# One flag for the instruction scheduler of a two-layer decoder trunk

## The chip, the cores and the metric

The kernel runs on one core of a Trainium2 chip. The metric is the device time of one execution in microseconds. Before the change the median is 2463.65 us over two runs (2462.15 and 2465.15).

## What is computed

The reference is a decoder trunk of two layers over 1024 tokens of width 1024, all in float32. Each layer normalises, mixes tokens in two ways side by side on 512 columns each, projects and adds; then a squared-ReLU MLP of width 4096 follows.

```python
for i in range(DEPTH):                      # DEPTH = 2
    u = rms_norm(h, norm_mix[i])
    if i % 2 == 0:  mix = mixer_fox_ssd(u, ...)   # forgetting attention (8 heads of 64) || Mamba-2 SSD
    else:           mix = mixer_sb_gla(u, ...)    # stick-breaking attention (8 heads) || gated linear attention
    h = h + mix
    u = rms_norm(h, norm_mlp[i])
    h = h + squared_relu_mlp(u, w_mlp_up[i], w_mlp_down[i])
return rms_norm(h, norm_final)
```

Forgetting attention (FoX here) is a softmax of scores plus a running sum of log gates. Stick-breaking attention multiplies the sigmoid of a score by the product of one minus the sigmoids of the later keys. SSD and gated linear attention (GLA) carry a state from chunk to chunk.

## The kernel before, in words

Every float32 product is made of three matmuls on numbers split into a high and a low half: `split` (L78 on ACT, L79 on DVE) writes a rounded copy and the remainder, and `projA` (L146 to L158, matmuls on L156) and `mulB` (L165 to L174, matmuls on L172) multiply high by high, high by low and low by high over eight blocks of 128 rows. One product of 128 by 512 is thus 24 matmuls into one bank of PSUM.

In order of time, with the times of the profile, the stages are: norm and value projection (to 67 us), forgetting attention (67 to 281), convolution projections of SSD (to 365), the SSD loop over eight chunks (to 475), output projection (to 548), MLP (to 1195; up part at L414, down part at L572), value projection of layer 1 (to 1247), stick-breaking attention (1262 to 1495), GLA projections (to 1590), GLA (to 1730), output projection (to 1800), MLP (to the end).

Both attentions run through `attend` (L222). It takes four pairs of heads. For each pair it projects queries and keys (`qk_pair`, 96 matmuls on L156 in four groups of 24), and then goes through four phases, two heads by two halves of the rows. A phase makes scores (L248 and L250, from the split keys `kh` and `kl` into a bank `sc`), probabilities (`rows`, on DVE, ACT and POOL, into tiles `pr`), and for the phase before it `weigh`: transposes (L273, into a bank `tr`), a split of them (L78, L79), and the product with the values (L265, into the bank `av`):

```python
for p in range(4):
    qkt = self.qk_pair(w, p * P, HF + p * P)
    for e in range(2):
        for hf in (1, 0):
            probs = self.scores(qkt, 2 * p + e, e, hf, rows)
            if last: self.weigh(pool, v, catT, *last)
            last = (p, e, hf, probs)
```

Queries and keys have one buffer each, so that the projections of a pair may run while the pair before it is still in work, but their results are written only when its last score has been made. In stick-breaking attention a row of 128 queries goes through two sigmoids on ACT (L874, L875), masks on POOL (L879), a running product on DVE (L881) and a multiplication on DVE (L882). In this text **stretch A** of a pair runs from the last score of the pair before to the last score of the pair's own first phase; **stretch B** holds the remaining three phases.

GLA handles each half of the tokens in two blocks of heads; each block goes through eight levels (`intra`, 16 small matmuls on L966 into two banks `sc`, then two copies under a mask on DVE, L973; before them L983 to L990 make the operands on POOL, ACT and DVE), and then four chunks follow (L1005 to L1043). Each chunk also needs a gate, 24 matmuls on L172 with weights `zw`, which depends on nothing in the levels. The SSD loop has gate products of the same kind.

PSUM has eight banks, handed out by name: three `mm` (projections, gates), two `sc`, two `tr`, one `av`.

The program is written as one list of instructions. The framework puts them into an order for each engine with a list scheduler: it models how long each instruction takes and what it waits for, and at each step picks one that could start. Each engine then works through its own list in that order, and waits on semaphores where an operand or a buffer isn't ready. So which matmuls stand between two scores is the scheduler's decision, not the program's.

## Time and profile before

| | us |
|---|---|
| median of the runs | 2463.65 |
| profiled execution, its own time | 2468.61 |
| its span | 2466.9 |
| TensorE busy in the span | 2386.3 (97%) |
| DVE busy | 1651.6 (67%) |
| ACT busy | 1285.7 (52%) |

The profile is of one execution; its own time stands 5 us over the median of the runs. Busy time of TensorE (PE) is modelled from the ends of pipelined matmuls, and a PE that is busy isn't PE at its peak. The stages differ in what limits them, so the rows below are taken by stretches.

### The profile page before, as it was taken

The page shows a single profiled execution, that of the slowest core. Times are in us where ns is not written, and L with a number is a line of the kernel's source. Part 1 is how long each engine was busy: PE and PEld are TensorE (multiplying, and loading weights), DVE is VectorE, ACT ScalarE, POOL GpSimd, SP SyncE. Part 2 cuts the span into 40 slices and gives each one's busy share as a digit, 9 for nine tenths or more (in the row PEclk, how much of TensorE's full clock was granted, in tenths as well). Part 3 has the DMA queues.
Part 4 walks back from the last instruction along what each step waited for, and adds up shares of the span by engine and source line. Part 5 has one row for each costly group of instructions (what it writes and reads, how often), then busy time and mean ns, then how long its engine had stood idle before and what let it go on. Part 6 is the DMA issues. An engine that isn't in the chain of part 4 may idle for free.

```text
span 2466.9 us, 35276 instructions
## 1 busy us (share of the span) xinstructions
PE 2386.3 (97%) x12350; PEld 1949.8 (79%) x12350; DVE 1651.6 (67%) x2972; ACT 1285.7 (52%) x2502; POOL 220.0 (9%) x310
## 2 busy tenths in 40 slices
PE   8999998999999999999998889999999999999998
PEld 7777776897888887888876668777988888888886
DVE  5687766557566658667659885577386655578567
ACT  4476636435555543445546664654155555544445
POOL 1011102100000000000013331122000000000000
PEclk9999998899999999999999999999999999999999
DMA  5211323203444478567511111101404444587576
GB/s 143 61 57 54 102 54 78 73 22 116 141 142 155 163 275 277 146 223 224 172 35 27 27 35 44 44 10 38 134 22 154 160 152 145 192 304 236 166 225 214
DMA packets 251586, 310.85 MB, mean 126 GB/s; under 512 B 24432, under 2 KB 148352, under 8 KB 251408
## 3 DMA queue, kind: packets, MB, share of 16 engines
q1 hardware_dynamic: 251408, 308.60, 39.2%
q8 instruction: 97, 1.59, 0.3%
q14 instruction: 81, 0.66, 0.1%
HBM read 237.16 MB, written 71.37 MB: 125 GB/s over the span
## 4 chain that ended last, share of the span: by engine, by line
PE 78%; issue 7%; DVE 6%; DMA 3%; POOL 3%; ACT 2%; SPq 0%; POOLq 0%; DVEq 0%; ACTq 0%
PE tr L414 14%; PE mm L572 10%; PE mm L172 9%; PE mm L156 8%; PE sc L414 7%; PE mm L414 5%; PE sc L572 5%; PE tr L572 5%; PE sc L172 4%; PE av L572 3%; PE sc L966 2%; PE av L172 2%; PE av L265 1%; PE tr L273 1%; DVE rr L881 1%
## 5 line engine op out<-in xcount | busy, mean ns | idle before, releaser
L78 ACT CAST wh<-f 128x512 fp32r<-128x512 f32 (+1 forms) x384 | 224.3, 585 | 404.8 <-PE av L572 162.6
L79 DVE TENSOR_TENSOR wl<-f,wh 128x512 fp32r<-128x512 f32 (+1 forms) x384 | 246.6, 643 | 166.6 <-ACT wh L78 163.6
L79 DVE TENSOR_TENSOR wl<-raw,wh 128x512 fp32r<-128x512 f32 (+1 forms) x340 | 233.4, 689 | 123.4 <-ACT wh L78 119.5
L78 ACT CAST wh<-raw 128x512 fp32r<-128x512 f32 (+1 forms) x340 | 209.4, 619 | 178.8 <-PE mm L414 47.0
L156 PE MATMUL mm<-U,wh 128*128 128x512 f32 x832 | 279.3, 404 | 0.0
L172 PE MATMUL mm<-wh,U 128*128 128x256 f32 (+2 forms) x992 | 227.8, 313 | 0.2 <-ACT U L78 0.2
L414 PE MATMUL tr<-E,wh 128*128 128x512 f32 x720 | 225.5, 394 | 0.0
L156 PEld LDWEIGHTS mm<-U,wh 128*128 128x128 f32 x832 | 156.8, 191 | 31.6 <-issue 0.8
L123 POOL TENSOR_TENSOR rs<-ms,mhalf 128x1 f32<-128x1 f32 (+2 forms) x56 | 41.8, 748 | 1552.8 <-DVE ms L121 1552.8
L172 PEld LDWEIGHTS mm<-wh,U 128*128 128x128 f32 x992 | 163.4, 190 | 14.6 <-issue 4.0
L156 PE MATMUL mm<-U,wl 128*128 128x512 f32 x416 | 167.9, 404 | 0.0
L414 PEld LDWEIGHTS tr<-E,wh 128*128 128x128 f32 x720 | 135.4, 188 | 31.7
L172 PE MATMUL mm<-wl,U 128*128 128x256 f32 (+2 forms) x496 | 154.3, 311 | 0.6 <-DVE wl L79 0.6
L572 PE MATMUL mm<-wl,wh 128*128 128x512 f32 x384 | 152.3, 397 | 0.3 <-DVE wl L79 0.2
L572 PE MATMUL mm<-wh,wh 128*128 128x512 f32 x384 | 151.4, 394 | 0.0
L572 PE MATMUL mm<-wh,wl 128*128 128x512 f32 x384 | 151.2, 394 | 0.0
L414 PE MATMUL sc<-U,wh 128*128 128x512 f32 x480 | 150.4, 394 | 0.0
L414 PE MATMUL tr<-E,wl 128*128 128x512 f32 x360 | 141.9, 394 | 0.0
L78 ACT CAST ph<-tr 128x512 fp32r<-128x512 f32 x192 | 88.7, 487 | 64.0 <-PE tr L273 62.3
L273 PE MATMUL tr<-ident,pr 128*128 128x128 f32 x576 | 96.9, 278 | 21.2 <-DVE pl L79 16.0
L172 PE MATMUL sc<-wh,U 128*128 128x256 f32 (+1 forms) x560 | 108.7, 285 | 0.2
L414 PE MATMUL mm<-U,wh 128*128 128x512 f32 x304 | 99.3, 405 | 8.2 <-ACT U L78 7.1
(343 smaller groups left out, 5638.1 us busy)
## 6 DMA issues: line engine op xcount, KB each, us to landing
raw<-in_w_mlp_down SPq DMA_DIRECT2D x192, 256.0 KB, 3.8
raw<-in_w_mlp_up SPq DMA_DIRECT2D x128, 256.0 KB, 3.5
q<-in_w_mlp_down SPq DMA_DIRECT2D x64, 512.0 KB, 4.7
f<-hidS SPq DMA_DIRECT2D x128, 256.0 KB, 2.9
hidS<-q SPq DMA_DIRECT2D x96, 256.0 KB, 3.0
hidA<-f SPq DMA_DIRECT2D x64, 256.0 KB, 3.2
f<-hidA SPq DMA_DIRECT2D x64, 256.0 KB, 2.9
raw<-in_w_in_ab SPq DMA_DIRECT2D x40, 256.0 KB, 3.0
```

The lines of the kernel that those rows point to most:

```text
L78: self.nc.scalar.copy(hi, src)
L79: self.nc.vector.tensor_tensor(out=lo, in0=src, in1=hi.bitcast(F32), op=ALU.subtract)
L123: nc.gpsimd.tensor_tensor(rs, ms, self.mhalf[:, :w], op=ALU.pow)
L156: nc.tensor.matmul(ps, a, b[hf][:, kc], start=kc == 0 and i == 0, stop=kc == NKC - 1 and i == 2)
L172: nc.tensor.matmul(d, a, b, start=kc == 0 and i == 0, stop=kc == NKC - 1 and i == 2)
L265: nc.tensor.matmul(av[:, o:], v[j][:, h], x[:, o:], start=j == 0 and k == 0, stop=j == nj - 1 and k == 1)
L273: nc.tensor.transpose(ps[:, k * P:(k + 1) * P], probs[k][:, j * P:(j + 1) * P], self.ident)
L414: nc.tensor.matmul(ps, a[:, kc], b[:, kc], start=new and kc == 0 and i == 0, stop=kc == 3 and i == 2, skip_group_check=True)
L572: nc.tensor.matmul(ps[j], l[:, cs], r, start=own is not None and k == 0 and x == 0, stop=k == NG - 1 and x == 2, skip_group_check=True)
L881: nc.vector.tensor_tensor_scan(s, s, s, 1.0, ALU.mult, ALU.bypass)
L966: nc.tensor.matmul(ps[hh][:, c], kx[rows, cs], qx[rows, cs], start=True, stop=True)
```

## The change

The context in which the program is scheduled gets one flag. The traced program is the same; the list scheduler takes its durations and waits from the framework's other timing model.

```diff
-    with tile.TileContext(nc) as tc:
+    with tile.TileContext(nc, schedule_with_timeline_sim=True) as tc:
         trunk(tc, *args)
```

What it changes is the order on each engine. ACT has two fewer loads of its function table (36 for 38); the instructions are otherwise the same ones. POOL's order differs in a few places, and SP, which issues the DMAs, has its issues moved by at most about 26 places.

In both attentions the projections of the next pair are placed otherwise. The first place is PE in stretch B of stick-breaking attention, between two pieces of scores of a phase (`sc_13681` and `sc_13741` are banks of scores; `mm_13930` is a projection of the next pair). Before:

```order
L248 MATMUL sc_13681<-kh_3005_13212,qs_3003_13210 128x512
L250 MATMUL sc_13681<-kl_2856_12574,qs_3003_13210 128x512
L265 MATMUL av_13697<-ph_13703,v_12082 128x512
L156 MATMUL mm_13930<-U_76,wh_13897 128x512
L156 MATMUL mm_13930<-U_76,wl_13898 128x512
L156 MATMUL mm_13930<-U_76,wh_13897 128x512 x2
L156 MATMUL mm_13930<-U_76,wl_13898 128x512
L156 MATMUL mm_13930<-U_76,wh_13897 128x512
L248 MATMUL sc_13741<-kh_3005_13212,qs_3003_13210 128x128
L250 MATMUL sc_13741<-kl_2856_12574,qs_3003_13210 128x128
```

With the change, from the same score on:

```order
L248 MATMUL sc_13681<-kh_3005_13212,qs_3003_13210 128x512
L250 MATMUL sc_13681<-kl_2856_12574,qs_3003_13210 128x512
L265 MATMUL av_13533<-ph_13606,v_12089 128x128
L265 MATMUL av_13533<-pl_13607,v_12089 128x128
L273 MATMUL tr_13707<-ident_69,pr_3057_13494 128x128
L273 MATMUL tr_13707<-ident_69,pr_3060_13508 128x128
L273 MATMUL tr_13707<-ident_69,pr_3063_13522 128x128
L248 MATMUL sc_13741<-kh_3005_13212,qs_3003_13210 128x128
L250 MATMUL sc_13741<-kl_2856_12574,qs_3003_13210 128x128
L273 MATMUL tr_13715<-ident_69,pr_3060_13508 128x128
L273 MATMUL tr_13715<-ident_69,pr_3063_13522 128x128
```

The five projections that stood between the two scores are gone; transposes of the phase before stand there. All over stretch B it is 34 projections before and none now.

The second place is PE in stretch A, around the first score of the next pair (`sc_14036`). Before:

```order
L273 MATMUL tr_14119<-ident_69,pr_3133_13786 128x128
L156 MATMUL mm_14577<-U_76,wh_14567 128x512
L248 MATMUL sc_14036<-kh_3164_13887,qs_3162_13885 128x128
L156 MATMUL mm_14577<-U_76,wh_14567 128x512
L156 MATMUL mm_14577<-U_76,wl_14568 128x512
L156 MATMUL mm_14577<-U_76,wh_14567 128x512
L250 MATMUL sc_14036<-kl_2855_12573,qs_3162_13885 128x128
L248 MATMUL sc_14052<-kh_3164_13887,qs_3162_13885 128x512
L250 MATMUL sc_14052<-kl_2855_12573,qs_3162_13885 128x512
```

With the change:

```order
L156 MATMUL mm_14577<-U_76,wl_14568 128x512
L156 MATMUL mm_14577<-U_76,wh_14573 128x512 x2
L156 MATMUL mm_14577<-U_76,wl_14574 128x512
L156 MATMUL mm_14577<-U_76,wh_14573 128x512 x2
L156 MATMUL mm_14577<-U_76,wl_14574 128x512
L156 MATMUL mm_14577<-U_76,wh_14573 128x512 x2
L248 MATMUL sc_14036<-kh_3164_13887,qs_3162_13885 128x128
L156 MATMUL mm_14577<-U_76,wl_14574 128x512
L156 MATMUL mm_14577<-U_76,wh_14573 128x512
L250 MATMUL sc_14036<-kl_2855_12573,qs_3162_13885 128x128
```

The projections (`mm_14577`) now stand in blocks of one piece ahead of the score and between its two matmuls, where one to three stood before. Over a stretch A of stick-breaking attention it is 62 projections before (50 in the second pair's) and 96 now; in forgetting attention 68 and 96 in stretch A, 28 and none in stretch B. In the last pair of stick-breaking attention, which has no next pair, 75 more value projections of GLA (L172, 264 columns) stand inside the stage, and 54 instead of 129 behind it.

The third place is PE in GLA's levels (`sc_16205` to `sc_16241` are banks of levels, `mm_16472` is a gate product). Before, three gate matmuls stand between every two levels:

```order
L966 MATMUL sc_16205<-gM_16199 128x128
L966 MATMUL sc_16206<-gM_16199 128x128
L172 MATMUL mm_16472<-wh_16121,U_76 128x512
L172 MATMUL mm_16472<-wl_16122,U_76 128x512
L172 MATMUL mm_16472<-wh_16121,U_76 128x512
L966 MATMUL sc_16223<-gM_16217 128x128 x3
L966 MATMUL sc_16224<-gM_16217 128x128 x3
L966 MATMUL sc_16223<-gM_16217 128x128
L966 MATMUL sc_16224<-gM_16217 128x128
```

With the change a whole gate product of 24 stands ahead of each of the first levels of a half (`mm_16548` is one), and none from the sixth on; these are later levels:

```order
L966 MATMUL sc_16331<-gM_16325 128x128 x4
L966 MATMUL sc_16332<-gM_16325 128x128 x4
L966 MATMUL sc_16349<-gM_16343 128x128 x4
L966 MATMUL sc_16350<-gM_16343 128x128 x4
L966 MATMUL sc_16367<-gM_16361 128x128 x4
L966 MATMUL sc_16368<-gM_16361 128x128 x4
L966 MATMUL sc_16385<-gM_16379 128x128 x4
L966 MATMUL sc_16386<-gM_16379 128x128 x4
L966 MATMUL sc_16403<-gM_16397 128x128 x4
L966 MATMUL sc_16404<-gM_16397 128x128 x4
```

Nothing but the levels' own matmuls is left between these levels, where three gate matmuls stood. In the SSD loop the gate products move forward in the same way: 45 and 43 of the 512-column matmuls stand in the steps after the first two chunks, and 12 of 256 columns in each later step. In the MLPs the first product of a group is moved ahead of the later products of the group before it.

## Rows read from the trace of the kernel before

**Rows 1.** The page: span, busy time, granted clock of PE in 40 slices

```profile
span 2466.9 us, 35276 instructions
...
PE 2386.3 (97%) x12350; PEld 1949.8 (79%) x12350; DVE 1651.6 (67%) x2972; ACT 1285.7 (52%) x2502; POOL 220.0 (9%) x310
...
PEclk9999998899999999999999999999999999999999
```

**Rows 2.** Windows: length, busy PE, PEld, DVE, ACT, POOL, clock, DMA share, GB/s

```profile
178.50:207.00 28.50, 28.19 (x144) 22.07 (x143) 20.96 (x50) 19.38 (x39) 2.11 (x5) 1.00 0.23 66
207.00:229.60 22.60, 22.29 (x125) 17.61 (x124) 20.52 (x68) 18.73 (x43) 5.54 (x11) 1.00 0.13 38
1368.50:1399.50 31.00, 27.95 (x138) 20.73 (x137) 25.47 (x46) 20.09 (x43) 7.31 (x15) 1.00 0.13 35
1399.50:1429.20 29.70, 25.65 (x130) 18.31 (x129) 28.95 (x44) 21.13 (x50) 15.85 (x18) 1.00 0.07 19
600.00:900.00 300.00, 300.00 (x1294) 242.90 (x1293) 176.92 (x274) 163.22 (x275) 0.00 (x0) 1.00 0.49 163
381.60:464.60 83.00, 78.49 (x390) 57.42 (x390) 61.88 (x122) 53.85 (x129) 25.35 (x25) 0.89 0.24 58
...
430.50:437.20 6.70, 4.41 (x19) 2.37 (x18) 2.65 (x9) 5.01 (x11) 3.84 (x4) 1.00 0.25 46
437.20:444.00 6.80, 6.80 (x26) 5.97 (x25) 4.78 (x8) 4.13 (x12) 1.09 (x1) 0.50 0.21 33
...
1260.00:1495.00 235.00, 207.66 (x1067) 154.88 (x1065) 206.57 (x332) 157.95 (x352) 85.63 (x127) 1.00 0.10 27
1590.00:1730.00 140.00, 136.50 (x959) 105.22 (x957) 99.39 (x207) 68.16 (x182) 34.85 (x33) 1.00 0.10 30
```

**Rows 3.** Windows of one pair of each attention, projections on L156 alone

```profile
178.50:207.00 28.50, 18.25 (x69) 12.68 (x69) 1.00 0.23 66
207.00:229.60 22.60, 8.30 (x28) 4.85 (x27) 1.00 0.13 38
1368.50:1399.50 31.00, 16.99 (x62) 11.05 (x61) 1.00 0.13 35
1399.50:1429.20 29.70, 10.75 (x35) 6.59 (x36) 1.00 0.07 19
```

**Rows 4.** Chain of waits in saturated stretches: start, length, what ran

```profile
602.92 5.58 PE tr L414 x24
...
1207.52 2.85 PE mm L172 x24
```

**Rows 5.** PE in time, three GLA levels and the gate matmuls between two

```profile
1600.11 1.67 PE L966 MATMUL sc<-gM 64*128 64x128 f32 x16
1601.70 0.50 PE L172 MATMUL mm<-wh,U 128*128 128x512 f32 x1
1602.04 0.39 PE L172 MATMUL mm<-wl,U 128*128 128x512 f32 x1
1602.27 0.40 PE L172 MATMUL mm<-wh,U 128*128 128x512 f32 x1
1602.60 1.59 PE L966 MATMUL sc<-gM 64*128 64x128 f32 x16
...
1605.02 1.65 PE L966 MATMUL sc<-gM 64*128 64x128 f32 x16
```

**Rows 6.** Groups of DVE, 1589.5 to 1628.7: busy, mean ns of one, idle

```profile
L973 DVE COPY_PREDICATED v<-kl,sc 128x512 f32<-128x512 int32 x27 | 18.2, 728 | 0.4 <-PE sc L966 0.4
L988 DVE TENSOR_TENSOR gM<-gM,v 128x256 f32<-128x256 f32 x14 | 5.9, 424 | 5.1 <-ACT gM L986 5.1
L990 DVE TENSOR_TENSOR gM<-gM,v 128x256 f32<-128x256 f32 x14 | 5.9, 420 | 0.0
```

**Rows 7.** Waits of PE: us in total, times, longest

```profile
PE tr L273 <- DVE pl L79: 16.0, 22, 1.5
PE mm L414 <- ACT U L78: 7.1, 4, 2.7
```

**Rows 8.** PE in time ahead of a fall of the clock, SSD loop

```profile
435.81 0.48 PE L786 MATMUL sc<-CT,BT 64*128 64x128 f32 x2 [1.94 <-DVE tmp L810]
```

## Prediction, made before the changed kernel was run

> **What bounds the kernel now.** I read the page first: PE is busy 2386.3 of a span of 2466.9 us, 97%, DVE 67%, ACT 52%, and PE's granted clock is near full in almost every slice [rows 1]. An order can't remove work, so what it can win is limited by PE time that isn't work. For that I priced PE's matmuls by stretches in which they stand back to back: 24 matmuls of 512 columns took 5.58 us, 0.232 each, and 24 of 256 columns 2.85 us, 0.119 each [rows 4]. Transposes and matmuls of 128 columns cost 0.10 to 0.11: sixteen in 1.59 to 1.67 us [rows 5].
>
> Next come the windows by stage [rows 2]. In 300 us of the MLP PE is busy for 300.00: whatever stands in whatever order there, the sum is the same. In forgetting attention PE is busy 28.19 of 28.50 and 22.29 of 22.60, so PE sets the pace in both stretches. In stick-breaking attention it is otherwise: in stretch A PE has 27.95 of 31.00 and DVE 25.47, in stretch B DVE has 28.95 of 29.70, 97%, and PE waits 4.05 us. Over the whole stage PE is idle 27.3 us of 235 [rows 2], and the waits name DVE's split of the transposed probabilities, 16.0 us in 22 waits [rows 7]. The SSD loop leaves PE idle 4.5 us of 83, and one stretch of 6.80 us ran at clock 0.50 [rows 2]. GLA leaves 3.5 of 140 [rows 2].
>
> So three stages have a second engine near its limit beside PE, and the filler (projections and gates that wait for nothing in the stage) is what lets PE and DVE be busy at the same time. Of projections the stretches hold 62 and 35 in stick-breaking attention, 69 and 28 in forgetting attention [rows 3].
>
> **The change, part by part.** It removes no matmul and adds none (the two table loads of ACT that go cost nothing gained, ACT being 52% busy [rows 1]). It moves filler. The moved order gives in stick-breaking attention 96 projections in stretch A and none in stretch B. I price each stretch by the larger of PE's work and DVE's.
>
> *Stick-breaking attention.* PE's work in A: 62 projections by 0.232, 14.4 us, and 11.1 us of scores, transposes and values, 25.5 before; with 96, 22.3 + 11.1 = 33.4. In B: 34 by 0.232, 7.9, and 14.4 of its own, 22.3 before; 14.4 after. DVE's work, at what its instructions take undisturbed, is some 20 in A and 27 to 29 in B, little changed. By the larger of the two, a pair takes 25.5 + 27.0 = 52.5 before and 33.4 + 29.1 = 62.5 after: 10 us more. But a pair is measured at 31.0 + 29.7 = 60.7 now [rows 2], so that it already pays 8.2 us of waits. If the new order has none of these, 62.5 is only 1.8 us more than 60.7. That is the lower bound of a boundary between pairs, 10 the upper one. There are three boundaries: +5 to +30. In the last pair the 75 GLA matmuls of 264 columns, 9.2 us by the 0.119 of 256 columns scaled, fill B's idle PE and are missing behind the stage: between 0 and -9.2. Together -4 to +30. I take 6 us for each boundary, the middle, because the 16.0 us of waits on DVE [rows 7] are a chain (transpose, split, values) that a block of filler doesn't shorten, and half of the 9.2; the first boundary gains 46 projections where the others gain 34, 2.8 us more, half of it taken: 18 - 4.6 + 1.4, **+15**.
>
> *Forgetting attention.* PE's work in A goes from 27.0 to 32.2, in B from 20.7 to 15.8, where DVE's 20.5 [rows 2] to 21.4 then decides. The larger-of sum goes from 48.4 to 53.6, +5.2 a boundary; against the measured 51.1 it is only +1.6 to +2.5. Three boundaries: +5 to +16, and +2 at the upper end for the first pair, whose first phase holds 72 projections in blocks. I take **+13**, near the upper end, since PE is saturated here now [rows 2] and has no waits to give up, and what 51.1 has over 48.4 will stay.
>
> *SSD loop.* The gate products come in large blocks after the first two chunks and thinly later. The larger-of sum over the chunks grows by 9; at the best PE's 4.5 us of gaps and 3.4 us (half of the 6.80 at clock 0.50) go away. Bounds -8 and +10; **+2**, because the chain between chunks and not the amount of filler makes the gaps.
>
> *GLA.* DVE needs two copies of 0.728 and two products of 0.42, 2.30 us, for a level [rows 6]; PE 1.67 for a level's matmuls and 0.7 for three gate matmuls [rows 5]. Before they are even. In the eleven levels that lose their filler PE waits for DVE, 2.30 - 1.67 = 0.63 each, 6.9 us; in the first five a block of 24 costs PE 5.6 and DVE waits. What the chunk part wins back, since its gates are already made, is at most the 3.5 us of idle [rows 2]. Bounds -3 and +11 (6.9 and as much again over a part of the second half); **+4**.
>
> *MLPs and joins.* The MLPs stay saturated. At the joins PE waits 7.1 us in four waits for the first split operand, the longest 2.7 [rows 7]; the next group's first product ahead of them may cover that. Bounds -9 (the 7.1 and some idle at a smaller join) and +6 (two more waits like the longest); **-2**. SP's issues move a little; the DMA share of the windows is 0.07 to 0.49 [rows 2], so that a transfer a few issues later is hidden by what is loaded ahead; without that cover it would be one more wait like the 2.7, within the +6.
>
> *The clock.* At 437 us the granted clock fell to 0.50, the lower of the two levels (1.2 GHz), for 6.8 us, after a stretch in which PE was busy 4.41 of 6.70 us [rows 2] and had waited 1.94 us at once [rows 8]. Stretch B of stick-breaking attention keeps 1.00 at 25.65 of 29.70 now; after the change it has 14.4 us of work in 29, and GLA's later levels 1.67 in 2.30. Such a fall costs half of 6.8, 3.4 us, where PE then sets the pace, as in the block that follows, and nothing where DVE does. Two falls that count: **+7**, bounds 0 and, with seven, +25.
>
> Sum: 15 + 13 + 2 + 4 - 2 + 7 = +39, with all lower ends -19 and all upper ends +100. The profiled execution is 2468.6 us, so 2507.6; it stands 5 us over the median, so **2503 us** for a median.
>
> **Rivals.** *The clock falls at most of the thin stretches.* For it: there is one fall after a stretch 66% busy [rows 2], and B would be at 50%. There are about twelve places (the ends of the four stretches B of each attention, two halves of GLA, two steps of SSD): twelve times 3.4 is 41, less the 7 in the sum, so 2503 + 34 = 2537. Against it: in all of the stick stage, with 27.3 of 235 us idle, the windows show 1.00. The Trainium skill ("TensorE: Matmul & The Clock Gate", A second HAM failure mode: psum-queue depth-cycling) says that frequent short idles of PE between groups of matmuls suffice to make the clock go back and forth. By that rule the stick stage before would already do so; its rows at 1.00 speak against it, the SSD rows for it.
>
> *The blocks are paid by waits that are there already.* The place is stretch A of stick-breaking attention: if DVE has 5.6 us of finished scores to work on (one block of 24 by 0.232) whenever a block of projections begins, it never starves, and the 8.2 us of waits of a pair vanish. From that point on all blocks go to their lower ends: stick -4, FoX +5, SSD -8, GLA -3, joins -2, clock 0: -12, or 2452. For it: B is already 97% DVE, so that taking filler out of it can cost nothing there. Against it: only two banks hold scores, and in A DVE is already idle 5.5 of 31.0 us with 62 projections. The skill's rule ("Perfetto Trace Analysis", Identifying the Most-Contended Engine) is to judge PE's headroom by the busy share of weight loads; here that is 20.73 of 31.0, 0.67, in stretch A against 242.90 of 300, 0.81, in the MLP, which would leave 4.4 us of room in A for the extra projections (31.0 times the difference of the shares). That speaks for this rival.
>
> *The known terms at their upper ends* without the clock: 2503 + 5 + 8 + 15 + 7 + 8 = 2546.
>
> **How the numbers follow.** Forecast 0.50 (0.40 of it within 2%, 0.10 above); the clock 0.26 (0.22 slower, 0.04 within); the blocks paid by old waits 0.18 (0.15 within, 0.03 faster, where the joins and the SSD loop give more too); upper ends 0.06 (0.05 slower). 2% of 2463.65 is 49 us, 2414 and 2513, about what a measurement of this kernel can tell from no change. Faster 0.03, within 0.60, slower 0.37. The range goes from 2446, which takes in the second rival and a little more at the joins, to 2550, which takes in the clock's 2537 and the upper ends. The forecast's own range is 2480 to 2525.
>
> **What the profile after would show.** In stick-breaking attention a stretch A of about 34 to 36 us with 96 projections and PE nearly always busy, DVE idle more than now, and a stretch B of about 29 with PE idle for half of it. In forgetting attention A near 32, B near 21. In GLA periods of 2.3 us for the later levels, and 7 for the first. The MLP windows unchanged at 300 of 300. The clock at 0.50 in parts of stretch B would tell for the first rival; a pair of 60 us or less in stick-breaking attention for the second. I would be wrong if the MLPs moved, if B took more than 31 us, for then the chain and not DVE's work sets it, or if A had its projections without DVE waiting.

## The result and the profile after

The changed kernel takes 2579.4 us, median of two runs (2578.29 to 2580.51), against 2463.65 before: a ratio of 1.047, interval 1.0425 to 1.0515, or 116 us slower. The forecast was 2503 with a range up to 2550. It had the right sign and a third of the size.

The page of the changed kernel, its span, busy time and the granted clock, answering to [rows 1]:

```profile
span 2578.8 us, 35337 instructions
...
PE 2435.6 (94%) x12350; PEld 2023.5 (78%) x12350; DVE 1673.3 (65%) x2972; ACT 1285.0 (50%) x2500; POOL 211.1 (8%) x310
...
PEclk9999999699999999999999889977898999999999
```

The span grew by 111.9 us. PE's idle time went from 80.6 us (2466.9 less 2386.3) to 143.2, and the row of the clock has dips that it did not have. The mean clock fell from 0.989 to 0.956. Since the clock has two levels, 1.00 and 0.50, the time at half clock is twice the missing share: 0.022 of 2466.9 us, 54 us, before and 0.088 of 2578.8, 227 us, now, in 30 stretches instead of 8. PE loses at most half of that time: 27 us before, 113 now, 86 more. What can be seen of it is less: the span is PE's busy time and its idle time, and with the same matmuls the busy time grew by 49.3 us (2435.6 less 2386.3) and the idle time by 62.6. The rest of the 86 must have fallen on waits, some of them hidden in what counts as busy.

Windows by stage, of the kernel before and then of the changed kernel (length, busy PE, PEld, DVE, ACT, POOL, clock, DMA share, GB/s). The stages are: up to the first score; forgetting attention to its last value matmul; from there to the first MLP matmul (convolutions, SSD, output projection); MLP; value projection; stick-breaking attention and GLA's projections; GLA and output projection; MLP.

```profile
0.00:99.30 99.30, 85.99 (x562) 77.67 (x563) 55.04 (x120) 41.71 (x80) 8.26 (x18) 0.97 0.41 116
99.30:294.40 195.10, 192.91 (x1018) 150.92 (x1017) 161.07 (x456) 146.18 (x310) 29.77 (x62) 1.00 0.17 49
294.40:559.30 264.90, 252.45 (x1538) 214.12 (x1537) 165.92 (x283) 122.54 (x257) 37.41 (x39) 0.95 0.25 71
559.30:1198.10 638.80, 634.04 (x2745) 511.19 (x2746) 426.68 (x684) 327.51 (x578) 5.56 (x7) 1.00 0.58 191
1198.10:1269.80 71.70, 70.17 (x498) 65.52 (x498) 26.13 (x48) 22.80 (x46) 3.65 (x4) 1.00 0.25 74
1269.80:1591.10 321.30, 292.69 (x1558) 226.44 (x1558) 243.06 (x408) 204.00 (x430) 89.66 (x131) 0.99 0.13 34
1591.10:1825.60 234.50, 229.83 (x1749) 198.17 (x1747) 151.54 (x302) 99.40 (x238) 38.72 (x40) 1.00 0.15 49
1825.60:2457.90 632.30, 628.25 (x2696) 505.73 (x2695) 418.63 (x669) 319.41 (x562) 5.89 (x7) 1.00 0.58 190
```

```profile
0.00:93.70 93.70, 83.47 (x554) 77.70 (x555) 54.87 (x117) 40.33 (x77) 7.30 (x16) 0.98 0.40 111
93.70:325.10 231.40, 207.91 (x1040) 164.62 (x1038) 165.82 (x460) 148.42 (x312) 29.83 (x64) 0.96 0.17 46
325.10:606.20 281.10, 250.92 (x1519) 216.77 (x1520) 169.40 (x282) 121.80 (x254) 38.18 (x39) 0.90 0.24 66
606.20:1244.10 637.90, 633.08 (x2750) 513.14 (x2748) 432.17 (x686) 327.26 (x581) 6.74 (x7) 0.99 0.58 191
1244.10:1313.80 69.70, 69.70 (x499) 65.52 (x498) 26.27 (x48) 23.35 (x47) 3.90 (x4) 1.00 0.26 76
1313.80:1651.20 337.40, 299.19 (x1557) 243.19 (x1558) 240.54 (x408) 204.58 (x430) 78.68 (x131) 0.93 0.13 33
1651.20:1934.10 282.90, 260.39 (x1747) 232.91 (x1746) 156.89 (x301) 98.00 (x235) 39.87 (x41) 0.87 0.13 41
1934.10:2569.20 635.10, 630.87 (x2700) 509.70 (x2698) 423.64 (x670) 319.09 (x564) 5.52 (x6) 0.99 0.57 189
```

Row against row: start -5.6, forgetting attention +36.3, SSD and output projection +16.2, MLP -0.9, values -2.0, stick-breaking attention +16.1, GLA +48.4, MLP +2.8 (and 0.6 at the end). The loss is in the four stages with filler, and in these the clock fell: to 0.96, 0.90, 0.93 and 0.87. The MLPs, as saturated as before, hardly moved. By the rows PE's idle and busy time grew by 21.3 and 15.0 us in forgetting attention (some 5 of the 15.0 are 22 more matmuls), by 9.6 and 6.5 in stick-breaking attention and by 17.8 and 30.6 in GLA; in SSD the idle time grew by 17.7 and the busy time fell by 1.5. Waits and clock have thus a different share in each.

The stretches of a pair, answering to [rows 2] and [rows 3]: stick-breaking attention, A and B of the third pair, first all engines and then the projections alone (length, busy PE, PEld, clock, DMA share, GB/s).

```profile
1426.60:1463.70 37.10, 36.18 (x172) 30.03 (x172) 26.31 (x44) 19.83 (x42) 6.00 (x14) 0.92 0.14 36
1463.70:1492.20 28.50, 20.47 (x94) 14.53 (x94) 27.89 (x46) 21.48 (x52) 12.99 (x20) 0.85 0.04 10
```

```profile
1426.60:1463.70 37.10, 24.91 (x96) 18.19 (x96) 0.92 0.14 36
1463.70:1492.20 28.50, 0.00 (x0) 0.00 (x0) 0.85 0.04 10
```

A holds all 96 projections and takes 37.1 instead of 31.0 us; B holds none and takes 28.5 instead of 29.7, with DVE busy 27.89 of them. The pair is 65.6 against 60.7.

In forgetting attention the three pairs up to each next pair's first phase, and the last pair (before, they took 56.6, 51.1, 51.0 and 36.4 us):

```profile
93.70:174.20 80.50, 73.78 (x349) 58.63 (x348) 51.96 (x140) 47.16 (x94) 9.74 (x21) 0.94 0.21 58
174.20:232.20 58.00, 52.53 (x267) 42.13 (x266) 41.92 (x116) 38.12 (x80) 7.17 (x16) 0.97 0.18 47
232.20:289.30 57.10, 51.48 (x264) 41.64 (x263) 42.55 (x116) 38.02 (x80) 7.77 (x16) 0.97 0.16 46
289.30:325.10 35.80, 30.12 (x164) 22.22 (x162) 29.38 (x88) 25.13 (x58) 5.15 (x11) 0.95 0.09 18
```

PE was idle 0.6 us of a middle pair and is idle 5.6 now. The first pair holds 168 projections where it held 107, and the last pair 1 where it held 48: the first got longer by its work and more, and the last, with DVE busy 29.38 of 35.80, hardly got shorter.

In GLA, PE in time, answering to [rows 5]; first two levels with a block of gates between them, then the levels without gates, and a window of their matmuls alone:

```profile
1657.20 1.17 PE L966 MATMUL sc<-gM 64*128 64x128 f32 x16
...
1663.60 1.17 PE L966 MATMUL sc<-gM 64*128 64x128 f32 x16
...
1697.57 12.31 PE L966 MATMUL sc<-gM 64*128 64x128 f32 x70 [0.90 <-DVE v L973]
```

```profile
1698.70:1712.30 13.60, 13.60 (x77) 13.60 (x75) 0.50 0.01 2
```

A level is eight matmuls, each of which leaves two records; the counts are of records. The first levels come 6.4 us apart, a block of 24 gate matmuls between them. Later 70 records of levels run for 12.31 us without a wait, 0.176 us each, where sixteen took 1.59 to 1.67, 0.10 each, before: PE is busy all the time, and but for the first 1.1 us at half clock.

In the SSD loop, PE in time, the waits of PE there for this bank (us in total, times, longest), and ACT and DVE in time:

```profile
408.66 0.79 PE L172 MATMUL mm<-wh,U 128*128 128x512 f32 x1 [7.35 <-DVE zs L771]
```

```profile
PE mm L172 <- DVE zs L771: 11.3, 5, 7.3
```

```profile
405.32 0.42 ACT L822 ACTIVATE cd<-acb 64x4 f32<-64x4 f32 x2 [5.17 <-DMA acb<-acd]
407.29 1.09 ACT L770 ACTIVATE zs<-mm 128x512 f32<-128x512 f32 x2
407.92 1.28 DVE L771 TENSOR_TENSOR zs<-zs,mm 128x512 f32<-128x512 f32 x2 [2.43 <-ACT zs L770]
```

A gate product stands at the head of PE's list and waits 7.35 us for one of the three `mm` banks. Such a bank is free when ACT has taken the sigmoid of an earlier gate (L770) and DVE has multiplied by it (L771). ACT's sigmoid comes late because in ACT's list it stands behind a row of the chunk (L822) that waits 5.17 us for a load of `acb`. PE takes its list in order, so the chunk's own matmuls wait behind the gate, and the clock is at half when it goes on (from 405.1 us). This wait is thus made by PE's order together with ACT's and the time of a load. With SSD's order on PE alone (below) the longest wait for such a bank is 6.3 us.

### The profile page after: what moved, and what is told of

The parts are those of the page before. It is cut to its first block, busy times and chain, and to the rows that moved or that the text cites. A ratio compares the mean times of both kernels' runs of the same rounds, so it can differ in the third digit from the quotient of the medians.

```text
span 2578.8 us, 35337 instructions
## 1 busy us (share of the span) xinstructions
PE 2435.6 (94%) x12350; PEld 2023.5 (78%) x12350; DVE 1673.3 (65%) x2972; ACT 1285.0 (50%) x2500; POOL 211.1 (8%) x310
## 3 DMA queue, kind: packets, MB, share of 16 engines
q8 instruction: 97, 1.59, 0.3%
## 4 chain that ended last, share of the span: by engine, by line
PE 83%; DVE 7%; ACT 3%; issue 3%; DMA 2%; POOL 1%; SPq 0%; POOLq 0%; ACTq 0%; DVEq 0%
PE tr L414 13%; PE mm L156 11%; PE mm L572 10%; PE mm L172 8%; PE sc L414 6%; PE sc L572 5%; PE tr L572 5%; PE mm L414 5%; PE sc L172 4%; PE av L572 3%; PE av L265 2%; PE av L172 2%; PE sc L966 2%; PE tr L273 2%; DVE rr L881 1%
## 5 line engine op out<-in xcount | busy, mean ns | idle before, releaser
L156 PE MATMUL mm<-U,wh 128*128 128x512 f32 x832 | 272.1, 403 | 7.3 <-DVE kl L200 4.1
L172 PE MATMUL mm<-wh,U 128*128 128x256 f32 (+2 forms) x992 | 233.7, 320 | 13.5 <-DVE zs L771 11.3
L172 PEld LDWEIGHTS mm<-wh,U 128*128 128x128 f32 x992 | 172.5, 198 | 29.8 <-DVE zs L771 13.2
L156 PEld LDWEIGHTS mm<-U,wh 128*128 128x128 f32 x832 | 157.4, 192 | 45.3 <-DVE kl L200 5.4
L156 PE MATMUL mm<-U,wl 128*128 128x512 f32 x416 | 166.5, 400 | 0.0
L172 PE MATMUL mm<-wl,U 128*128 128x256 f32 (+2 forms) x496 | 156.6, 316 | 0.0
L273 PE MATMUL tr<-ident,pr 128*128 128x128 f32 x576 | 107.8, 299 | 22.0 <-DVE pl L79 10.4
L79 DVE TENSOR_TENSOR pl<-tr,ph 128x512 fp32r<-128x512 f32 x192 | 102.4, 547 | 30.8 <-ACT ph L78 30.2
L172 PE MATMUL sc<-wh,U 128*128 128x256 f32 (+1 forms) x560 | 114.4, 293 | 5.7 <-ACT U L78 5.5
L572 PE MATMUL mm<-wh,wh 128*128 128x512 f32 x384 | 115.9, 395 | 0.0
```

What stands on the lines that cost most here:

```text
L79: self.nc.vector.tensor_tensor(out=lo, in0=src, in1=hi.bitcast(F32), op=ALU.subtract)
L156: nc.tensor.matmul(ps, a, b[hf][:, kc], start=kc == 0 and i == 0, stop=kc == NKC - 1 and i == 2)
L172: nc.tensor.matmul(d, a, b, start=kc == 0 and i == 0, stop=kc == NKC - 1 and i == 2)
L273: nc.tensor.transpose(ps[:, k * P:(k + 1) * P], probs[k][:, j * P:(j + 1) * P], self.ident)
L572: nc.tensor.matmul(ps[j], l[:, cs], r, start=own is not None and k == 0 and x == 0, stop=k == NG - 1 and x == 2, skip_group_check=True)
```

## The experiments

**How an order is held.** A function behind the traced program ties instructions of one engine into a chain by edges of issue order only, after a table that was taken from another kernel's order. The table may hold all of an engine or only the matmuls of one stage. "Old model" and "new model" name the timing model of the scheduler, without the flag and with it. What a table does not hold the scheduler orders anew around it, and that is the limit of these experiments: a held engine meets others that aren't those of the kernel it came from. The code is shortened; how the tables are unpacked is left out.

```diff
         trunk(tc, *args)
+        pin(tc, nc)
...
+def pin(tc, nc):
+    at = {i.name: i for i in nc.cur_bb.bb.instructions}
+    info = mybir.DependencyInfo(mybir.DependencyClass.NoSync, mybir.DependencyReason.DATA)
+    for row in ORDERS:
+        for a, b in zip(row, row[1:]):
+            tc.add_manual_dep(at[b], a, info, reason="pin")
```

The theory was that filler on PE makes the loss. The rival was that the other engines' orders do. A run of the kernel before stands beside each experiment; its median was 2466.5 to 2468.6 in these sessions, and differences are to that.

**PE alone put back** (new model; table: all of PE, from before).

> The changed kernel (new timing model) with TensorE held to its order of before by a chain of issue order; all other engines keep what the new model gives them. Theory one, the place of the filler matmuls on PE is the whole cause: 2464 within 10 us, and half-clock time back near 53 us (before 53, changed kernel 228). Rival, the order on DVE, ACT and SP is the cause: over 2520.

It took 2553.45 us, ratio 1.0349 (1.0324 to 1.0374), 85 us slower than before. The theory fell and the rival's range held: PE's order gives back only a quarter. But this does not price the changed kernel's own orders on DVE and ACT, since the scheduler made new ones around the held PE: of DVE's 2972 rows at most 2403 stand here in the changed kernel's order and 2434 in that of before (between those two kernels it is 2240). In this kernel PE has the order of before, matmul for matmul, and waits in stick-breaking attention like this (waits of PE, this kernel, then the kernel before, whose 16.0 us on the split ahead of L273 stand in [rows 7]):

```profile
PE av L265 <- DVE pl L79: 12.9, 8, 2.8
PE tr L273 <- DVE pr L882: 9.3, 5, 2.5
PE tr L273 <- DVE pl L79: 6.7, 8, 2.7
```

```profile
PE av L265 <- DVE pl L79: 2.0, 4, 0.7
...
PE tr L273 <- DVE pr L882: 2.0, 2, 1.8
```

Two kinds of wait grew and one shrank; PE's idle time in the stage (with GLA's projections) is 41.2 us for 28.6. DVE has the same work in another order. One of the longer waits, on PE and on DVE:

```profile
1356.48 0.39 PE L265 MATMUL av<-pl,v 128*128 128x256 f32 x1 [2.23 <-DVE pl L79]
```

```profile
1354.67 1.30 DVE L191 SCALAR_TENSOR_TENSOR qs<-mm,qs 64x512 fp32r<-64x512 f32 x2
```

The split that PE needs (`pl`) begins only at 1356.00 us, behind rows of the scan and two rows for the next pair's queries (L191), though the high half that it reads was there at 1352.90. GLA's stage, which has no such pairs, got longer too with PE's order put back, by 23.6 us:

```profile
1647.80:1905.90 258.10, 244.06 (x1749) 207.84 (x1745) 152.70 (x300) 98.41 (x236) 38.61 (x40) 0.94 0.13 45
```

**PE's new order alone** (old model; table: all of PE, from the changed kernel).

> The kernel before (old timing model) with TensorE held to the order of the changed kernel. Theory one, filler on PE: 2579 within 15 us. Rival, the other engines' order: under 2500.

2630.12 us, ratio 1.0659 (1.0630 to 1.0688): beyond the range of either side, and worse than the changed kernel, whose other engines were ordered along with PE. So PE's new order is enough for a loss without the new model elsewhere, and the engines' orders can't be judged one by one.

**Two and three engines put back** (new model; tables of before for PE and DVE; PE and ACT; PE, DVE and ACT).

> The changed kernel with PE and DVE both held to their order of before; ACT, POOL and SP keep what the new model gives them. With PE alone held it took 2553. If DVE's order is what was left of the loss: 2464 to 2475. If ACT's order or the order of the loads on SP is: 2530 to 2555.

> The changed kernel with PE and ACT held to their order of before, DVE, POOL and SP as the new model has them. With PE alone 2553, with PE and DVE 2507. If DVE's order holds the larger part: 2510 to 2555. If ACT's does: 2464 to 2500.

> The changed kernel with PE, DVE and ACT held to their order of before; only the order of the DMA issues on SP and a few rows on POOL are the new model's. If the loss is made by the three compute engines' orders together: 2464 to 2475. If the loads' order holds a part of what was left with PE and DVE held (2507): 2490 to 2510.

| held as before | us | ratio to before |
|---|---|---|
| none (the change) | 2579.4 | 1.0470 (1.0425 to 1.0515) |
| PE | 2553.45 | 1.0349 (1.0324 to 1.0374) |
| PE, ACT | 2533.59 | 1.0271 (1.0234 to 1.0308) |
| PE, DVE | 2507.01 | 1.0164 (1.0132 to 1.0197) |
| PE, DVE, ACT | 2475.92 | 1.0035 (1.0017 to 1.0054) |

With PE's order back, DVE's gives 46 us more, which fits neither range, and ACT's 31 more on top of that (20 without DVE's). With all three back 8 us are left, one more than the range allowed, for the order of DMA issues and of POOL. All but these 8 us are made by the order on the three compute engines together.

**One other engine's new order alone** (old model; PE as before, and DVE or ACT as in the kernel with PE put back under the new model).

> The kernel before (old model) with PE held to its own order and DVE held to the order that it has in the kernel with PE alone held under the new model; ACT and SP follow from the old model. DVE's order is the cause: 2540 to 2560, with the SSD loop some 19 us and stick-breaking attention some 18 us longer than before. ACT's or the loads' order: below 2480.

> The kernel before (old model) with PE held to its own order and ACT held to the order that it has in the kernel with PE alone held under the new model. DVE's order is the cause: 2464 to 2480. ACT's order is: over 2530.

2625.6 us (1.0641, 1.0598 to 1.0683) and 2560.16 us (1.0375, 1.0335 to 1.0416). Either engine's order hurts by itself: DVE's by more than expected, ACT's where a time near that of before was expected. Both kernels are slower than the 2553 in which these two orders stand together; they show a dependence and are no price.

**One stage's filler alone** (old model; table: the matmuls of one stage, from the changed kernel; the other engines follow).

> The kernel before with only GLA's matmuls (its projections, levels, chunks and gates) held to the order of the changed kernel. From the two traces by stage GLA and what follows up to the next MLP is 35 us longer in the changed kernel: 2464 + 35 to 45 = 2499 to 2509, with 50 to 70 us at clock 0.50 there. If the 35 us come from the waits alone, the same time with less than 15 us at 0.50. If GLA's loss hangs on what the attention left behind: under 2480.

> The kernel before with only the attentions' matmuls (scores, transposes, values, projections of queries and keys) held to the order that the changed kernel has on PE; the rest of PE and the other engines follow from the old model. If the place of the projections is what costs in the attentions, the changed kernel's two stages are +48 us and the time 2512 or, as in the kernel with the whole new order on PE under the old model, +84 and 2548. If DVE's order under the new model is what costs there and the place of projections nothing: under 2480.

> The kernel before with only the matmuls of the SSD loop (gates, chunks) held to the changed kernel's order on PE. The changed kernel's SSD stage is 26 us longer and the one behind it 8 shorter. If the gates' early place costs that: 2477 to 2492. If the order of ACT and DVE under the new model does: under 2470.

GLA 2510.53 us, ratio 1.0174 (1.0150 to 1.0199), 42 us, just above its range; both attentions 2536.25, 1.0278 (1.0239 to 1.0318), 69 us, between the two values expected; SSD 2486.91, 1.0075 (1.0049 to 1.0102), 20 us, within its range. Here PE's order does harm in each stage; the three add up to 131 us, more than the change. GLA's stage in its kernel:

```profile
1585.50:1865.10 279.60, 262.33 (x1750) 232.45 (x1747) 155.04 (x302) 102.97 (x240) 38.59 (x40) 0.86 0.12 41
```

That is 279.6 us for 234.5, at clock 0.86, nearly what the changed kernel has there (282.9 at 0.87). The other engines stayed almost as they were (2912 of 2972 rows of DVE and 2447 of 2502 of ACT stand in the order of before). So in GLA the order on PE, which moves the gates, is enough to make the loss. It isn't the only order that can: with PE put back the stage still took 23.6 us more, as shown above. PE in time in the kernel with GLA's new order, the first of the levels without gates and the first behind the clock's fall at 1630.4 us:

```profile
1620.77 1.71 PE L966 MATMUL sc<-gM 64*128 64x128 f32 x16
...
1630.38 15.26 PE L966 MATMUL sc<-gM 64*128 64x128 f32 x80 [0.86 <-DVE v L973]
```

Four levels lie between these two, in 9.61 us at full clock, 2.40 each; behind the fall five take 15.26, 3.05 each, without a wait.

**Clock or waits, in GLA** (the kernel with GLA's new order; three extra matmuls ahead of each of 24 levels without gates, once of 512 columns, once of the level's own kind; `pf` and `ps` are the level's two score banks, and the last line stands in the second kernel in place of the matmul above it).

```diff
+            if 16 * hf + 8 * i + lev in (*range(6, 21), *range(23, 32)):
+                for k in range(3):
+                    nc.tensor.matmul(pf[0], zw[0][0][:, :P], zw[0][0], start=True, stop=True)
...
+                    nc.tensor.matmul(ps[0][:, 0], kx[:64, :P], qx[:64, :P], start=True, stop=True)
```

> The kernel before with GLA's matmuls in the changed kernel's order (2510 by itself), and three extra matmuls of 128 rows by 512 columns ahead of each of the 24 levels that have no gate matmuls beside them; their result is overwritten. 72 matmuls, 16.7 us of PE work. Theory, the clock: the levels' own small matmuls alone don't hold it (it fell after 7 us of them with waits of 0.3 us), so that a level takes 3.2 us at half clock and 2.4 with the extra work at full clock: the 35 us lost at half clock in GLA shrink under 15, and the time falls to 2485 to 2500 although PE does more. Rival, the levels wait for DVE: no gain, 2510 to 2527.

> As the kernel with 72 extra matmuls of 512 columns, but the extra matmuls are three of the level's own kind (64 rows, 128 columns, float32) ahead of each of the same 24 levels, 15 us of PE work at full clock. Theory, the clock isn't held by this kind of work: it stays at 0.50 in the levels and the extra work costs double, 2525 to 2540. Rival, any PE work that closes the waits holds the clock: 2485 to 2500. Rival, the levels wait for DVE: 2510 to 2515.

2505.46 us (1.0150, 1.0114 to 1.0185) and 2522.33 us (1.0218, 1.0183 to 1.0253). Windows of the whole stage and of a run of late levels, of the kernel without extra matmuls (its whole stage stands above; here the levels just ahead of the clock's fall and those behind it), with those of 512 columns, and with the small ones:

```profile
1623.00:1630.40 7.40, 6.21 (x53) 5.40 (x52) 4.90 (x10) 1.44 (x4) 2.52 (x3) 1.00 0.00 0
1630.40:1648.40 18.00, 18.00 (x96) 17.14 (x96) 12.63 (x25) 4.42 (x12) 5.56 (x6) 0.50 0.00 1
```

```profile
1588.00:1863.30 275.30, 256.55 (x1822) 220.03 (x1820) 154.21 (x302) 102.54 (x240) 40.15 (x40) 0.96 0.13 42
...
1634.00:1652.00 18.00, 16.17 (x124) 12.55 (x124) 13.04 (x26) 4.77 (x14) 6.30 (x6) 1.00 0.01 1
```

```profile
1585.80:1877.70 291.90, 277.82 (x1894) 250.26 (x1892) 155.58 (x302) 102.99 (x240) 39.91 (x40) 0.86 0.12 40
...
1636.00:1660.00 24.00, 24.00 (x128) 23.28 (x128) 12.36 (x23) 4.42 (x12) 6.18 (x6) 0.50 0.00 1
```

About as much extra work (16.7 us by 0.232 each; the small ones 15 by two records of 0.104 each) gives two different clocks: with 512 columns PE works at 1.00 and the stage is 4.3 us shorter than without, with small matmuls it stays at 0.50 and the stage is 12.3 longer. That the clock is on the path of GLA's late levels is thus shown, and the 16.6 us between the two stages are its net price here, as far as the two fillers are alike: the small ones also read the level's own operands, but in the window shown PE was busy 24.00 of 24.00 us and waited for none. The small filler met its range; with 512 columns the time stayed above the 2485 to 2500 expected. PE in time, two levels of the kernel with 512 columns, says why:

```profile
1641.37 0.97 PE L967 MATMUL sc<-wh 128*128 128x512 f32 x3 [0.36 <-DVE v L979]
1642.27 1.71 PE L972 MATMUL sc<-gM 64*128 64x128 f32 x16
1644.24 0.96 PE L967 MATMUL sc<-wh 128*128 128x512 f32 x3 [0.27 <-DVE v L979]
```

A level comes every 2.87 us: the extra matmuls go into the score bank, so that they wait for DVE's copy out of it (L979 is L973 here) and the level waits for them. The gates of the kernel before stand in the same place but go into their own banks, off that chain, and a level takes 2.42 to 2.49 [rows 5].

**The same in the attentions** (the kernel with their new order; one matmul of 512 columns ahead of each score of stretch B).

> The kernel before with the attentions' matmuls in the changed kernel's order (2536 by itself, 37 us lost at half clock in the two stages and 72 us of waits), and one extra matmul of 128 rows by 512 columns ahead of each score of the three later phases of a pair, its result overwritten: 128 matmuls, 30 us of PE work. If the clock's falls in the stretches without projections lie on the path: half the 37 us come back, and with waits filled the time is 2520 to 2540 in spite of the work. If DVE alone sets those stretches and the clock costs nothing: the extra work is hidden too, 2536 to 2545, and the time lost at half clock may fall with no gain. If PE's work decides: 2550 to 2566.

2543.49 us, ratio 1.0311 (1.0268 to 1.0354), 7 us more than without; the two runs lie 9 us apart. The stages, forgetting attention and stick-breaking attention with GLA's projections without the extra matmuls, and forgetting attention with them:

```profile
97.40:326.70 229.30, 204.66 (x1017) 162.46 (x1017) 163.76 (x456) 147.10 (x310) 30.30 (x62) 0.94 0.15 42
1299.90:1653.20 353.30, 306.23 (x1558) 247.07 (x1558) 244.43 (x408) 205.30 (x430) 88.05 (x131) 0.91 0.12 31
```

```profile
96.10:325.20 229.10, 208.08 (x1070) 166.43 (x1069) 164.28 (x455) 147.29 (x310) 29.02 (x62) 0.98 0.15 41
```

In forgetting attention the clock rises from 0.94 to 0.98, PE does 53 matmuls more by the trace's records, and the time is the same; stick-breaking attention takes 360.5 us, 7.2 more, with the clock at 0.93. The whole time lies in the range expected if DVE sets these stretches and the clock costs nothing. But 53 matmuls are 12.3 us of work by 0.232, and PE's busy time grew by 3.4: work paid by the clock fits as well. Which of the two it is stays open.

**More filler in the changed kernel** (new model, its own order on PE; two extra matmuls ahead of each score of stretch B, three ahead of the last eleven levels of each half).

> The changed kernel in its own order on PE, with extra matmuls of 512 columns whose result is overwritten: two ahead of each score of the three later phases of a pair in both attentions, three ahead of each of the last eleven levels of each half of GLA; 322 matmuls, 75 us of PE work. If the loss is the clock (97 us of the changed kernel's span is lost at half clock, 22 before): stick-breaking attention and GLA keep clock 1.00, some 50 us of loss go, the extra work costs up to 15 where PE already sets the pace: about 2540 to 2550. If the loss is DVE's starving in the blocks: no gain, 2580 to 2600.

2608.85 us, ratio 1.0573 (1.0547 to 1.0599): 29 us more than the change, for 75 us of work, and above both ranges. The clock went from 0.956 to 0.973, which is some 43 us less lost at half (0.044 of 2578.8, 113, against 0.027 of 2608.3, 70). The work cost more than that gave back.

**Filler in the kernel before's SSD loop** (old model, PE as before; 22 extra matmuls where PE waits ahead of the first chunk, three in each of the last three).

> The kernel before in its own order on PE, with extra matmuls of 128 rows by 512 columns whose result is overwritten, in the SSD loop alone: 22 ahead of the first chunk's L798, where PE waits 6 us for DVE, and three ahead of those of the last three chunks, where the clock fell at 437 and 451 us. If an early fall of the clock there costs what rows say (8.3 us lost at half clock): 5 to 9 us faster, 2456 to 2460, though PE does 7 us more. If not, 0 to 3 us slower.

2473.80 us, ratio 1.0029 (1.0011 to 1.0046): 7 us slower, outside both ranges. In the profiled execution, one of the faster ones, the stage took 268.7 us for 264.9 while its clock rose from 0.95 to 0.97. The 31 extra matmuls are 7.2 us of work by 0.232, and PE's busy time in the stage grew by only 2.6: the clock gave some of it back, and no time was won. What a fall of the clock alone costs there isn't shown. No kernel here beats the one before.

## Why the prediction was wrong

The terms of the sum came to +39; the change cost 116 us. The step that failed is the price of a stretch, the larger of PE's work and DVE's at full clock. It left out that each engine takes its own list in order and waits at a row that isn't ready, and that PE can work at half clock while it is busy. PE's idle time grew by 62.6 us and its busy time by 49.3, for the same matmuls.

- **The change part by part** priced PE's order alone and gave the orders of DVE and ACT no cost, since their work was the same. With PE's order back 85 us remain, and DVE's and ACT's orders give back all but 8 of them: equal work in another order is not equal time. But PE's order alone, stage by stage, already costs 42, 69 and 20 us, so the terms below were too small by themselves. How the changed kernel's 116 us divide among the three engines stays open.
- **The clock, +7 with two falls,** was mis-sized. There were 22 more stretches at half clock than before, up to 20.5 us long, where each fall was priced at 6.8 (the longest before was 13.7), worth at most 86 us against the +25 of my upper end. I looked for falls after waits of PE [rows 8]. In GLA the clock fell after such waits too (PE busy 6.21 of 7.40 us), but it stayed at half while PE was busy 18.00 of 18.00. The first rival named the mechanism, and its sign came (0.85 in stretch B); it stood at 2537 with falls of one length. How much of the 86 us lies on the path is shown for GLA's late levels alone, 16.6 us net between two kinds of extra work. The Trainium skill ("TensorE: Matmul & The Clock Gate", A second HAM failure mode: psum-queue depth-cycling) tells of frequent short idles between groups of matmuls with which the clock goes back and forth. The stretches B and the fall in GLA agree with it, since there PE had short waits; the 18.00 us at half clock with PE busy throughout are not covered by it.
- **GLA, +4,** came out at +48.4, and at +45.1 in its stage with GLA's order on PE alone. I took the later levels at DVE's 2.30 us, with PE at full clock. In the kernel with that order four levels without gates took 2.40 us each while the clock was full, so this step held until the clock fell. At half clock a level's matmuls take 3.0 us (18.00 by 16/96), and PE, not DVE, sets it. The first half's levels with the 24 gate matmuls came 6.4 us apart, less than the 7 expected. Of the 48.4 us, 30.6 are more busy time of PE for the same matmuls, and 17.8 more idle time.
- **Forgetting attention, +13,** came out at +36.3. The two later boundaries cost 6.9 and 6.1 us (58.0 for 51.1, 57.1 for 51.0), over the 5.2 of the upper end. The first, put at no more than 5.2 and 2 for the first pair, cost 23.9: 61 projections more are 14.2 us by 0.232, PE was idle 6.7 us instead of 0.6, and the clock was 0.94. What they left behind gave next to nothing back: the last pair has 47 fewer and took 35.8 us for 36.4.
- **SSD, +2,** came out at +16.2, past the upper end of 10, and at 18.9 in its stage with SSD's order on PE alone. I counted the work of the blocks against DVE and forgot the banks: gate products fill the three `mm` banks, the next waits 7.35 us until ACT and DVE have worked off one, and what the chunk needs stands behind it.
- **Stick-breaking attention, +15,** came out at +16.1, near in size. Its stretches came about as told: A 37.1 with 96 projections and B 28.5 with none, where 34 to 36 and 29 were expected; PE idles 8.0 us of B, less than half, with the clock at 0.85. That the whole stage fits is in part luck: with the attentions' new order on PE under the old model it took 353.3 us for 321.3, 32 more, and a fall of the clock was priced in another term.
- **MLPs and joins, -2,** was right: -0.9, -2.0 and +2.8.
- **The second rival** (blocks paid by old waits, 2452) fell: idle time of PE grew. The rule that it was stood beside (the Trainium skill, "Perfetto Trace Analysis", Identifying the Most-Contended Engine) judges PE's headroom by the busy share of its weight loads or by its share of peak work; from the first I estimated 4.4 us of room in stretch A. There 34 more projections, 7.9 us of work by 0.232, cost 6.1 us, and PE's idle time fell from 3.05 to 0.92: about 2 us of room.

## What to carry to other kernels

When a scheduler reorders everything, price every engine's order, not only the bottleneck's: put back one engine at a time, then two, then three, before believing any single cause, and compare what the scheduler made of the engines that were left free. In this kernel filler was best between the steps of a chain, a few matmuls at a time and into banks of its own; packed in blocks it took banks, stood ahead of work in an in-order list, and left stretches in which the clock dropped. At a long wait follow the releaser one step further: behind the wait for DVE stood ACT, and behind ACT a load. Read the granted clock beside the busy share: a PE that is busy all the time can be at half speed.

## What the runs showed of the hardware

- PE kept busy by GLA's level matmuls alone (64 rows, 128 columns, float32) stayed at clock 0.50: 18.00 of 18.00 us, and 24.00 of 24.00 with more of them. With three matmuls of 512 columns ahead of each level it ran at 1.00, although it was busy only 16.17 of 18.00.
- A gain in clock need not be a gain in time: in the SSD loop the clock went from 0.95 to 0.97 with 7.2 us more work, and the stage got 3.8 us longer; in forgetting attention it went from 0.94 to 0.98 with 53 matmuls more, and the time was the same.
